# Two-layer adaLN trunk on one core: odd shift blocks of the first stage summed by VectorE, x multiplied by the norm's rows on GpSimd

## The chip, the cores and the metric

The kernel runs on one core of one Trainium2 chip. The metric is the device time of one execution in microseconds (us), as the median of several runs. The engines are named as in the profile: PE (TensorE matmul), PEld (its weight loads), DVE (VectorE), ACT (ScalarE), POOL (GpSimd) and SP (SyncE), which issues the loads.

## The reference

A trunk of two layers over 256 positions and 1024 features, batch 1. Each sub-layer is `x + gate(c) * f(rmsnorm(x) * gain * (1 + scale(c)) + shift(c))`. Layer 0 has block-sparse causal attention with 8 heads of 128 (with 256 positions and blocks of 256 it is one causal block), layer 1 a short gated convolution of width 3; each is followed by a SwiGLU with 2816 hidden features. Shift, scale and gate of each sub-layer are six vectors of 1024 per layer:

```python
sc = jax.nn.silu(c)
for i in range(DEPTH):
    mod = sc @ w_ada[i] + b_ada[i]
    sh_m, sc_m, g_m, sh_f, sc_f, g_f = jnp.split(mod, 6, axis=-1)
    h = modulate(x, norm_mix[i], sh_m, sc_m)   # rms_norm(x, gain) * (1 + scale) + shift
    ...
```

All is float32. The change touches only the first of these: shift and scale of layer 0's mixer, and the h that goes into q and k.

## The kernel before

**Layout.** x is held with features on the 128 partitions, as eight blocks of 128 features x 256 positions (`xT[:, k]`, k = 0 to 7). Matrix products are made in three passes of a split of both operands into a high part (rounded to fp32r) and the rest: `mm3` (lines 252 to 258) issues high x high, high x low and low x high.

**The first stage** (lines 554 to 629) computes q and half of k, 1536 columns, straight from the input. It runs over the eight feature blocks k, not over column chunks, since block k of the normed input h needs shift and scale of block k alone, and these come out of `c` and weights that are still on their way. Six PSUM accumulators (`accs`, four for q, two for k) take 12 groups of three products from each block, 36 products per step.

The order of PE, DVE and ACT is written out by hand here (`manual_schedule`, line 554); POOL and SP are ordered by the framework. In the loop at line 602, step k issues block k's products, with the work for block n = k+1 put in between:

- Loads on SP: the scale block n, the weight rows `wf_qk_n` (lines 138 to 141), and with even n the two shift blocks n and n+1 together. Shift and scale blocks are of 512 KB; two of a kind share one of five 1 MB buffers (tag `wf`), in which the weight rows lie as well. A load waits until the buffer that it gets has been read for the last time. The framework hands the buffers out.
- `scale_column` (line 494): the scale block lies turned, with the output features on the partitions, so one DVE instruction multiplies it by a row of silu(c) that is the same on all partitions (`c_all`) and sums along the free axis (`ada_sum`, line 107). `scale_of` (line 490) then adds the bias and multiplies by the gain.
- `mod_sums` (line 463) for the shift: the block lies with the input features on the partitions, and PE multiplies it by columns of silu(c), to four partial rows. For n = 1 it takes one block (128 columns); for n = 2, 4 and 6 it takes two, n and n+1 (256 columns). ACT copies the rows out of PSUM (line 473), and `mod_columns` (line 476) turns them into a column by products with `firsts`. `shift_columns` (line 484) has ACT add the bias for each column.
- `w_operands` and `operands` (lines 514 and 520): in three pieces of 512 columns, ACT rounds the weight rows to `wh` (line 511) and DVE forms the rest `wl` (line 512).
- `normed` (line 499): DVE forms t = xT x scale column x rows0 in one instruction. `rows0` is the reciprocal root mean square of each position, the same on all partitions.
- `h_operand` (line 504): ACT adds the shift and rounds to `m0h` (line 505), DVE forms the rest `m0l` (line 506).

```python
for k in range(KD):
    n = k + 1
    ...
    first_products(k, ops, range(0, ja))
    if sums:
        y = mod_sums(shifts[:, 1:2] if n == 1 else shifts, f"sh{n}")
    if n < KD:
        scale_column(scales[:, n % 2], n)
    first_products(k, ops, range(ja, jb))
    if n < KD:
        ops_n = w_operands(n, wf)
        if sums:
            shift_columns(y, n)
        t = normed(n)
    first_products(k, ops, range(jb, 6))
    if n < KD:
        operands(n, t, wf, ops_n)
```

So DVE's order for block n is ada_sum, scale_of, wl(0:2), t, m0l, wl(2:4), wl(4:6). In the texts "step n" is this work for block n; PE's products of block n come after it.

After the stage the rest of q, k and v, attention and all further layers follow, with weight chunks of 1 MB split by ACT (line 98) and DVE (line 99), and with further `ada_sum` pieces (line 109) for the later shifts, scales and gates.

Of the kernel before, what the change touches and what calls it, by code (L numbers as in the profile page):

```python
# [11 lines left out]
AF = mybir.ActivationFunctionType  # L12
# [4 lines left out]
S = 256  # L17
# [16 lines left out]
def trunk_kernel(ctx: ExitStack, tc: tile.TileContext, x_t, cols_in, scale_in, shift_in, ada_in, qk_rows, kv_in, o_in,  # L34
# [87 lines left out]
    def mcol(l, part, k):  # L122
        i = l * 48 + part * KD + k
        return mod[:, i:i + 1]
# [20 lines left out]
    def room(tag, n, name, dtype=F32):  # L145
        size = {"al": KF * S + 16, "ah": KF * S, "zh": KD * (S + 32), "zl": KD * (S + 2)}.get(tag, KD * S)
        return act.tile([P, size], dtype, tag=tag, name=name)[:, 16 if tag == "al" else 0:][:, :n]
# [4 lines left out]
    def new_pair(tag, name, nk):  # L152
        return tuple(pair_rows(room(tag + p, nk * S, name + p, F32R)) for p in "hl")

    room("al", 1, "first_al")
    xT = act.tile([P, KD, S], F32, name="xT")
    hs = new_pair("h", "m0", KD)
    room("ah", 1, "first_ah")
# [304 lines left out]
    def mod_sums(w, name):  # L463

        n = w.shape[1]
        ps = ps_misc("mod_ps_" + name)[:, :n * P]
        for k in range(KD):
            g = 32 * (k % 4)
            nc.tensor.matmul(ps[g:g + 32].rearrange("p (n c) -> p n c", c=P), sc[:, k:k + 1].to_broadcast([P, 32]),
                             w[:, :, k * P:(k + 1) * P], start=k < 4, stop=k >= 4, skip_group_check=True,  # L470
                             tile_position=(0, g))
        y = tmp.tile([P, 2 * P], F32, tag="t", name="mod_y_" + name, bufs=3)[:, :n * P]
        nc.scalar.activation(y, ps, AF.Copy)
        return y

    def mod_columns(y, name):

        ps = ps_misc(f"mod_c_{name}")
        n = y.shape[1] // P
        for i in range(n):  # L480
            nc.tensor.matmul(ps[:, i:i + 1], y[:, i * P:(i + 1) * P], firsts, start=True, stop=True)
        return ps[:, :n]

    def shift_columns(y, k):
        ps = mod_columns(y, f"sh{k}")
        for n in range(ps.shape[1]):
            nc.scalar.activation(mcol(0, SH_M, k + n), ps[:, n:n + 1], AF.Identity,
                                 bias=b_cols[:, SH_M * KD + k + n:][:, :1])

    def scale_of(m, k, sums):  # L490

# [2 lines left out]
    def scale_column(w, k):  # L494
        m = mcol(0, SC_M, k)
        ada_sum(m, w, f"sc{k}")
        scale_of(m, k, m)

    def normed(k):
        t = tmp.tile([P, S], F32, tag="t", name=f"t_m0_{k}", bufs=3)  # L500
        nc.vector.scalar_tensor_tensor(t, xT[:, k], mcol(0, SC_M, k), rows0, op0=ALU.mult, op1=ALU.mult)
        return t

    def h_operand(k, t):
# [34 lines left out]
    def keep_warm(n):  # L539

        ps = ps_misc("warm")
        for _ in range(n):
            nc.tensor.matmul(ps[:, :2 * P].rearrange("p (n c) -> p n c", c=P), ident_r,
                             ident_r.unsqueeze(1).to_broadcast([P, 2, P]), start=True, stop=True, skip_group_check=True)
# [9 lines left out]
    with tc.manual_schedule(engines={mybir.EngineType.PE, mybir.EngineType.DVE, mybir.EngineType.Activation}):  # L554
        nc.vector.tensor_copy(ident_r, ident)
        nc.vector.tensor_copy(mask_r, causal)

        std = const.tile([P, 2], F32, name="std0")
        nc.scalar.activation(std[:, :1], eps, AF.Silu)
        keep_warm(4)  # L560
        nc.scalar.activation(sc, c_cols, AF.Silu)
        nc.scalar.activation(std[:, :1], eps, AF.Sqrt)
        b_one = const.tile([P, KD], F32, name="b_one")
        nc.vector.tensor_scalar(b_one, b_cols[:, SC_M * KD:][:, :KD], 1.0, None, op0=ALU.add)
        nc.vector.tensor_scalar(qg, v_cols[:, 56:57], HD ** -0.5, None, op0=ALU.mult)

        c_ps = [ps_alt(f"c_ps_{i}") for i in range(2)]
        for k in range(KD):
            nc.tensor.matmul(c_ps[k // 4][:, k % 4 * P:][:, :P], sc[:, k:k + 1].to_broadcast([P, P]), ident, start=True,
                             stop=True)  # L570
        keep_warm(6)
        sq = room("zl", RAW, "sq0")
        ssq = const.tile([P, 2], F32, name="ssq0")
        nc.scalar.activation(sq[:, :D], x_tok[:, 0], AF.Square, accum_out=ssq[:, 0:1])
        nc.vector.scalar_tensor_tensor(sq[:, D:2 * D], x_tok[:, 1], 1.0, x_tok[:, 1], op0=ALU.mult, op1=ALU.mult,
                                       accum_out=ssq[:, 1:2])
        for i in range(2):
            nc.scalar.activation(c_all[:, i * 512:(i + 1) * 512], c_ps[i], AF.Copy)
        nc.scalar.activation(std, ssq, AF.Sqrt, bias=eps, scale=1.0 / D)
        rstd0 = const.tile([P, 2], F32, name="rstd0")  # L580
        nc.vector.reciprocal(rstd0, std)
        x_ps = turn_x(0, ps_alt)
        nc.vector.tensor_copy(xT[:, 0:2], x_ps)
        y = mod_sums(scales[:, 0:1], "sc0")
        rr0 = rstd_rows(rstd0, "rr_0")
        rows0 = tmp.tile([P, S], F32, tag="rrow", name="rows0", bufs=1)
        nc.scalar.activation(rows0, rr0, AF.Copy)
        x_ps = turn_x(1, ps_alt)
        ps = mod_columns(y, "sc0")
        scale_of(mcol(0, SC_M, 0), 0, ps)  # L590
        y = mod_sums(shifts[:, 0:1], "sh0")
        t = normed(0)
        nc.vector.tensor_copy(xT[:, 2:4], x_ps)
        keep_warm(2)
        ops = w_operands(0, wf)
        shift_columns(y, 0)
        x_ps = [turn_x(i, ps_alt) for i in (2, 3)]
        operands(0, t, wf, ops)
        for i in range(2):
            nc.scalar.activation(xT[:, 4 + 2 * i:6 + 2 * i], x_ps[i], AF.Copy)  # L600
        keep_warm(4)
        for k in range(KD):
            n = k + 1
            if n < KD:
                if n % 2 == 0:
                    shifts, scales = ada_first(n // 2)
                    load_first(shifts, shift_in, n)
                    load_first(shifts, shift_in, n + 1)
                elif n == 1:
                    load_first(shifts, shift_in, 1)  # L610
                load_first(scales, scale_in, n)
                wf = first_rows(n)
            ja, jb = ((2, 3), (1, 2), (1, 4), (0, 3))[min(k, 3)]
            sums = n < KD and (n == 1 or n % 2 == 0)
            first_products(k, ops, range(0, ja))
            if sums:
                y = mod_sums(shifts[:, 1:2] if n == 1 else shifts, f"sh{n}")
            if n < KD:
                scale_column(scales[:, n % 2], n)
            first_products(k, ops, range(ja, jb))  # L620
            if n < KD:
                ops_n = w_operands(n, wf)
                if sums:
                    shift_columns(y, n)
                t = normed(n)
            first_products(k, ops, range(jb, 6))
            if n < KD:
                operands(n, t, wf, ops_n)
                ops = ops_n
# [193 lines left out]
def _lay_out(inputs):  # L823

    import numpy as np

    a = {k: np.asarray(v) for k, v in inputs.items()}

    def feats(v):
        return v.reshape(-1, P).T  # L830

    def chunks(w):

        k, j = w.shape[0] // P, w.shape[1] // CW
        return w.reshape(k, P, j, CW).transpose(2, 1, 0, 3).reshape(j, P, k * CW)

    ada = a["w_ada"].reshape(DEPTH, D, 6, KD, P)
    turned = ada.transpose(0, 2, 3, 4, 1)
    qkv = a["w_qkv"][0]

    def sums(part):

        return ada[0, :, part].reshape(KD, P, KD, P).transpose(2, 1, 0, 3).reshape(KD, P, D)

    return {
        "x_tok": a["x"][0].reshape(2, P, D).transpose(1, 0, 2),
        "cols": np.concatenate([feats(a[n]) for n in ("b_ada", "norm_mix", "norm_ffn", "conv_w", "q_gain", "k_gain", "c")],
                               axis=1),
        "scale": np.concatenate([sums(SC_M)[:1], turned[0, SC_M, 1:]]),
        "shift": sums(SH_M),  # L850
        "ada": turned.reshape(DEPTH, 6, 4, 2, P, D).transpose(0, 1, 2, 4, 3, 5).reshape(DEPTH, 6, 4, P, 2 * D),
        "qk_rows": qkv[:, :D + D // 2].reshape(KD, P, D + D // 2),
        "kv": chunks(qkv[:, D + D // 2:]),
        "o": chunks(a["w_o"][0]),
        "in": chunks(a["w_in"][0]),
        "out": chunks(a["w_out"][0]),
        "gate_up": np.stack([chunks(w) for w in a["w_gate_up"]]),
        "down": np.stack([chunks(w) for w in a["w_down"]]),
    }
# [21 lines left out]
```

## Time and profile before

| | us |
|---|---|
| median of 3 runs (586.2 to 587.33) | 587.23 |
| the profiled execution, its own time | 586.6 |
| its span in the trace | 584.8 |
| PE busy | 577.4 (99%) |
| DVE busy | 454.8 (78%) |
| ACT busy | 316.1 (54%) |
| POOL busy | 1.1 |

The span is what the trace covers; 1.8 us of the execution lie around it. Starts are in us from the start of the span. A row of the timeline gives start, duration, engine, line, operation, written and read tiles, their shapes and count, and in brackets an idle time before it with what ended it. Durations of instructions that follow each other on an engine overlap a little, so the distance between two starts is what an instruction costs its engine.

### The profile page before, as it was taken

What the parts mean: (1) busy time and instruction counts of PE and PEld (TensorE: products, weight loads), DVE (VectorE), ACT (ScalarE), POOL (GpSimd) and SP (SyncE); (2) the same over time, 40 slices, a digit from 0 to 9 for tenths busy, and PEclk for the clock granted to TensorE, in tenths of its full rate; (3) what the DMA queues carried; (4) which work ended last, traced back from release to release, by engine and by line L of the source; (5) the groups of instructions that cost most, each with busy time, mean ns of one, the idle gap of its engine ahead of it and who ended that gap; (6) DMA issues with size and microseconds to landing.
All of it is one profiled execution on the core that took longest, in us unless ns stands there. A gap on an engine that the chain in (4) does not pass through costs nothing.

```text
span 584.8 us, 12020 instructions
## 1 busy us (share of the span) xinstructions
PE 577.4 (99%) x5032; PEld 569.8 (97%) x5032; DVE 454.8 (78%) x722; ACT 316.1 (54%) x526; POOL 1.1 (0%) x8
## 2 busy tenths in 40 slices
PE   7999999999999999999999999999999999999997
PEld 6899999999999999999999999999999999999997
DVE  4789989999999798967977999759986576555550
ACT  6457889597644454544445745446745345443330
POOL 0000000000000000000000000000000000000000
PEclk9999999999999999999999999999999999999999
DMA  8999999955898999968986379637387566655400
GB/s 316 396 380 409 356 331 334 341 208 187 335 377 303 347 334 342 331 240 303 330 310 254 129 291 366 247 122 261 128 331 280 180 261 216 238 174 200 148 19 18
DMA packets 25109, 156.04 MB, mean 267 GB/s; under 512 B 2784, under 2 KB 3168, under 8 KB 8928
## 3 DMA queue, kind: packets, MB, share of 16 engines
q1 hardware_dynamic: 25056, 155.28, 71.8%
q8 instruction: 39, 0.64, 0.4%
q14 instruction: 14, 0.11, 0.0%
HBM read 154.22 MB, written 1.05 MB: 266 GB/s over the span
## 4 chain that ended last, share of the span: by engine, by line
PE 93%; DMA 2%; DVE 2%; ACT 1%; issue 1%; SPq 0%; ACTq 0%; DVEq 0%
PE pu L255 7%; PE pu L254 7%; PE pu L258 7%; PE op_d L255 6%; PE op_d L254 6%; PE op_d L258 6%; PE pg L254 6%; PE pg L258 6%; PE pg L255 6%; PE raw_f L254 1%; PE op_o L258 1%; PE raw_f L255 1%; PE raw_f L258 1%; PE pb L258 1%; PE pb L254 1%; PE op_o L254 1%
## 5 line engine op out<-in xcount | busy, mean ns | idle before, releaser
L109 DVE SCALAR_TENSOR_TENSOR prod<-wa,c_all 128x1024 f32<-128x1024 f32 x80 | 97.6, 1220 | 18.0 <-DMA wa<-in_ada_dram 17.2
L98 ACT ACTIVATE wh_d<-wf_d 128x1024 fp32r<-128x1024 f32 (+1 forms) x48 | 45.2, 981 | 62.6 <-issue 41.9
L99 DVE TENSOR_TENSOR wl_d<-wf_d,wh_d 128x1024 fp32r<-128x1024 f32 (+1 forms) x48 | 52.8, 1132 | 23.9 <-ACT wh_d L98 23.7
L98 ACT ACTIVATE wh_g<-wf_g 128x1024 fp32r<-128x1024 f32 x44 | 45.7, 1053 | 44.6 <-issue 44.2
L98 ACT ACTIVATE wh_u<-wf_u 128x1024 fp32r<-128x1024 f32 x44 | 44.6, 1051 | 36.1 <-issue 30.5
L99 DVE TENSOR_TENSOR wl_u<-wf_u,wh_u 128x1024 fp32r<-128x1024 f32 x44 | 52.3, 1220 | 13.6 <-ACT wh_u L98 13.3
L99 DVE TENSOR_TENSOR wl_g<-wf_g,wh_g 128x1024 fp32r<-128x1024 f32 x44 | 53.5, 1219 | 2.4 <-ACT wh_g L98 2.2
L254 PE MATMUL op_d<-a0h,wh_d 128*128 128x256 f32 x176 | 48.6, 276 | 0.0
L258 PE MATMUL op_d<-a0h,wl_d 128*128 128x256 f32 x176 | 48.6, 276 | 0.0
L255 PE MATMUL op_d<-a1l,wh_d 128*128 128x256 f32 x176 | 48.6, 276 | 0.0
L254 PE MATMUL op_d<-a1h,wh_d 128*128 128x256 f32 x176 | 48.6, 276 | 0.0
L255 PE MATMUL op_d<-a0l,wh_d 128*128 128x256 f32 x176 | 48.6, 276 | 0.0
L258 PE MATMUL op_d<-a1h,wl_d 128*128 128x256 f32 x176 | 48.6, 276 | 0.0
L254 PE MATMUL pg<-f0h,wh_g 128*128 128x256 f32 x160 | 44.5, 278 | 0.0
L258 PE MATMUL pg<-f0h,wl_g 128*128 128x256 f32 (+3 forms) x164 | 44.5, 275 | 0.0
L254 PE MATMUL pg<-f1h,wh_g 128*128 128x256 f32 x160 | 44.3, 277 | 0.0
L255 PE MATMUL pg<-f0l,wh_g 128*128 128x256 f32 x160 | 44.2, 276 | 0.0
L254 PE MATMUL pu<-f0h,wh_u 128*128 128x256 f32 x160 | 44.2, 276 | 0.0
L258 PE MATMUL pg<-f1h,wl_g 128*128 128x256 f32 x160 | 44.2, 276 | 0.0
L258 PE MATMUL pu<-f1h,wl_u 128*128 128x256 f32 x160 | 44.2, 276 | 0.0
L255 PE MATMUL pu<-f0l,wh_u 128*128 128x256 f32 x160 | 44.2, 276 | 0.0
L255 PE MATMUL pg<-f1l,wh_g 128*128 128x256 f32 x160 | 44.2, 276 | 0.0
(294 smaller groups left out, 2022.8 us busy)
## 6 DMA issues: line engine op xcount, KB each, us to landing
wa<-in_ada_dram SPq DMA_DIRECT2D x40, 1024.0 KB, 6.8
wf_g<-in_gate_up_dram SPq DMA_DIRECT2D x22, 1024.0 KB, 5.3
wf_u<-in_gate_up_dram SPq DMA_DIRECT2D x22, 1024.0 KB, 4.9
wf_d<-in_down_dram SPq DMA_DIRECT2D x16, 1024.0 KB, 6.1
wf_d<-in_down_dram SPq DMA_DIRECT2D x8, 768.0 KB, 5.3
wa_sc<-in_scale_dram SPq DMA_DIRECT2D x8, 512.0 KB, 6.9
wa_sh<-in_shift_dram SPq DMA_DIRECT2D x8, 512.0 KB, 7.9
wf_qk<-in_qk_rows_dram SPq DMA_DIRECT2D x8, 512.0 KB, 6.7
```

Of the source, the lines that this page charges most:

```text
L98: nc.scalar.activation(wh[:, a:b], wf[:, a:b], AF.Copy)
L99: nc.vector.tensor_sub(wl[:, a:b], wf[:, a:b], wh[:, a:b].bitcast(F32))
L109: nc.vector.scalar_tensor_tensor(t, w, 1.0, c_all, op0=ALU.mult, op1=ALU.mult, accum_out=dst)
L254: nc.tensor.matmul(ps, ah, bh, start=first, stop=False, skip_group_check=True)
L255: nc.tensor.matmul(ps, ah, bl, start=False, stop=False, skip_group_check=True)
L258: nc.tensor.matmul(ps[:, a:b], al, bh[:, a:b], start=False, stop=last, skip_group_check=True)
```

## The change

Shift blocks with odd n are laid out turned in memory, as the scale blocks are, and DVE sums them with `ada_sum`, ahead of the scale's. Shift blocks with even n stay on PE, one block (128 columns) at a time, and n = 1 leaves PE. A new tile `xn` holds x times rows0 for blocks 1 to 7; POOL makes these products once, ahead of the loop. `normed` for blocks 1 to 7 becomes one ACT instruction that multiplies `xn` by the scale column; block 0 keeps the DVE instruction. `shift_of` adds the shift's bias on ACT for one column. `xn` takes the place of a one-column placeholder in the buffer `al`, which attention uses later.

```diff
-    room("al", 1, "first_al")
+    xn = pair_rows(room("al", KD * S, "xn"))
...
+    def shift_of(k, sums):
+        nc.scalar.activation(mcol(0, SH_M, k), sums, AF.Identity, bias=b_cols[:, SH_M * KD + k:][:, :1])
+
     def shift_columns(y, k):
-        ps = mod_columns(y, f"sh{k}")
-        for n in range(ps.shape[1]):
-            nc.scalar.activation(mcol(0, SH_M, k + n), ps[:, n:n + 1], AF.Identity,
-                                 bias=b_cols[:, SH_M * KD + k + n:][:, :1])
+        shift_of(k, mod_columns(y, f"sh{k}"))
...
     def normed(k):
         t = tmp.tile([P, S], F32, tag="t", name=f"t_m0_{k}", bufs=3)
-        nc.vector.scalar_tensor_tensor(t, xT[:, k], mcol(0, SC_M, k), rows0, op0=ALU.mult, op1=ALU.mult)
+        if k == 0:
+            nc.vector.scalar_tensor_tensor(t, xT[:, k], mcol(0, SC_M, k), rows0, op0=ALU.mult, op1=ALU.mult)
+        else:
+
+            nc.scalar.activation(t, xn[:, k], AF.Copy, scale=mcol(0, SC_M, k))
         return t
...
             nc.scalar.activation(xT[:, 4 + 2 * i:6 + 2 * i], x_ps[i], AF.Copy)
+        for k in range(1, KD):
+            nc.gpsimd.tensor_mul(xn[:, k], xT[:, k], rows0)
         keep_warm(4)
...
-            sums = n < KD and (n == 1 or n % 2 == 0)
+
+            sums = n < KD and n % 2 == 0
             first_products(k, ops, range(0, ja))
             if sums:
-                y = mod_sums(shifts[:, 1:2] if n == 1 else shifts, f"sh{n}")
+                y = mod_sums(shifts[:, 0:1], f"sh{n}")
             if n < KD:
+                if n % 2:
+                    ada_sum(mcol(0, SH_M, n), shifts[:, 1], f"sh{n}")
                 scale_column(scales[:, n % 2], n)
             first_products(k, ops, range(ja, jb))
             if n < KD:
                 ops_n = w_operands(n, wf)
                 if sums:
                     shift_columns(y, n)
+                else:
+                    shift_of(n, mcol(0, SH_M, n))
                 t = normed(n)
...
-        "shift": sums(SH_M),
+        "shift": np.stack([turned[0, SH_M, k] if k % 2 else sums(SH_M)[k] for k in range(KD)]),
```

## Rows read from the trace of the kernel before

**Rows 1.** The page: the span, the busy time of each engine with its share of the span, and of the 40 slices the lines for PE's granted clock and for DMA, in tenths.

```profile
span 584.8 us, 12020 instructions
PE 577.4 (99%) x5032; PEld 569.8 (97%) x5032; DVE 454.8 (78%) x722; ACT 316.1 (54%) x526; POOL 1.1 (0%) x8
...
PEclk9999999999999999999999999999999999999999
DMA  8999999955898999968986379637387566655400
```

**Rows 2.** Busy time by stretch: the stretch in us and its length, busy time of PE, PEld, DVE, ACT and POOL with the number of instructions, PE's granted clock, the share of DMA and GB/s.

```profile
20.00:25.00 5.00, 5.00 (x51) 4.42 (x43) 2.94 (x6) 2.26 (x7) 0.00 (x0) 1.00 1.03 405
25.00:30.00 5.00, 4.95 (x48) 4.57 (x51) 4.26 (x10) 2.23 (x6) 0.00 (x0) 1.00 1.02 375
...
50.00:60.00 10.00, 10.00 (x90) 8.78 (x89) 9.79 (x12) 9.56 (x22) 0.00 (x0) 1.00 1.01 411
```

**Rows 3.** The chain that ended last, from 15 to 26 and from 49 to 54 us: start, time on the chain, what.

```profile
15.41 6.78 DMA wf_qk<-in_qk_rows_dram
...
22.21 0.64 ACT wh_qk L511
...
24.60 0.49 DVE m0l L506
...
25.14 0.39 PE pq L255
...
49.58 0.20 PE pq L255
...
53.69 0.57 PE q_sums L661 x8
```

**Rows 4.** The timeline of DVE in the first stage: the ada_sum of step 1 and of step 2, the whole step 3 up to the ada_sum of step 4, and m0l of step 7.

```profile
14.42 1.23 DVE L109 SCALAR_TENSOR_TENSOR prod_sc<-wa_sc,c_all 128x1024 f32<-128x1024 f32 x1
...
20.93 1.23 DVE L109 SCALAR_TENSOR_TENSOR prod_sc<-wa_sc,c_all 128x1024 f32<-128x1024 f32 x1 [1.02 <-DMA wa_sc<-in_scale_dram]
...
26.33 1.22 DVE L109 SCALAR_TENSOR_TENSOR prod_sc<-wa_sc,c_all 128x1024 f32<-128x1024 f32 x1
27.47 0.08 DVE L109 DVE_READ_ACCUMULATOR prod_sc<-wa_sc,c_all 128x1 f32 x1
27.59 0.22 DVE L492 SCALAR_TENSOR_TENSOR mod<-mod,b_one,cols 128x1 f32<-128x1 f32 x1
27.73 0.68 DVE L512 TENSOR_TENSOR wl_qk<-wf_qk,wh_qk 128x512 fp32r<-128x512 f32 x1
28.33 0.48 DVE L501 SCALAR_TENSOR_TENSOR t_m<-xT,mod,rows 128x256 f32<-128x256 f32 x1
29.44 0.48 DVE L506 SCALAR_TENSOR_TENSOR m0l<-t_m,mod,m0h 128x256 fp32r<-128x256 f32 x1 [0.64 <-ACT m0h L505]
...
31.17 1.22 DVE L109 SCALAR_TENSOR_TENSOR prod_sc<-wa_sc,c_all 128x1024 f32<-128x1024 f32 x1
...
48.85 0.48 DVE L506 SCALAR_TENSOR_TENSOR m0l<-t_m,mod,m0h 128x256 fp32r<-128x256 f32 x1 [0.64 <-ACT m0h L505]
```

**Rows 5.** ACT: from its timeline rows0, the shift columns of step 2, m0h of step 3 and, from attention's k, an accumulator read and the instruction that reads what it wrote; and of line 338 in the later layers the durations in ns (least, median, most), first and last start.

```profile
9.76 0.38 ACT L587 ACTIVATE rows<-rr 128x256 f32<-128x256 f32 x1
...
22.75 0.39 ACT L487 ACTIVATE mod<-mod_c_sh,cols 128x1 f32<-128x1 f32 x2
...
28.90 0.51 ACT L505 ACTIVATE m0h<-t_m,mod 128x256 fp32r<-128x256 f32 x1 [2.77 <-DVE t_m L501]
...
68.66 0.22 ACT L643 ACTIVATION_READ_ACCUMULATOR sqh<-pk 128x1 f32 x1
68.92 0.30 ACT L646 ACTIVATE sd<-ss,eps 128x4 f32<-128x4 f32 x1
...
L338 ACT ACTIVATE a0h<-xT,mod x8: 494/496/513, 117.5 to 130.7; 128x256 fp32r<-128x256 f32 x8
```

**Rows 6.** The timeline of PE: mod_sums and columns of the shift, the narrow form of step 1 and the wide form of step 4.

```profile
14.70 0.64 PE L469 MATMUL mod_ps_sh<-wa_sh,sc 128*32 128x128 f32 x16
...
16.09 0.28 PE L481 MATMUL mod_c_sh<-firsts,mod_y_sh 128*128 128x1 f32 x2
...
29.41 1.07 PE L469 MATMUL mod_ps_sh<-wa_sh,sc 128*32 128x256 f32 x16
...
32.64 0.50 PE L481 MATMUL mod_c_sh<-firsts,mod_y_sh 128*128 128x1 f32 x4
```

**Rows 7.** The timelines of POOL and DVE at the start: POOL's last instruction, and two casts of the same form on DVE.

```profile
1.35 0.29 POOL L77 TENSOR_SCALAR_AFFINE_SELECT causal<-causal 128x128 f32<-128x128 f32 x1
...
1.43 0.29 DVE L555 CAST ident_r<-ident 128x128 fp32r<-128x128 f32 x1
1.68 0.23 DVE L556 CAST mask_r<-causal 128x128 fp32r<-128x128 f32 x1
```

**Rows 8.** Two loads as SP issued them, each with the time from its issue to its landing: the scale of step 4, and the first piece of the weight rows of step 6 (durations in ns, then first and last start).

```profile
L132 SPq DMA_DIRECT2D wa_sc<-in_scale_dram x1: 327/327/327, 21.0 to 21.0; - x1
DMA to landing us min/median/max: 9.0/9.0/9.0
...
L140 SPq DMA_DIRECT2D wf_qk<-in_qk_rows_dram x1: 328/328/328, 36.1 to 36.1; - x1
DMA to landing us min/median/max: 4.1/4.1/4.1
```

## The prediction

> **What bounds it now.** The page comes first [rows 1]: TensorE (PE) is busy 577.4 of 584.8 us, the granted clock is full in every slice, and DMA is near its most in the first eight slices. So any time lost or won in the first stage stays lost or won: behind it PE has hardly a gap in which to catch up. An average over the span says nothing of who paces the first stage, so the next view is busy time by stretch [rows 2]. From 25 to 30 us PE is full, VectorE (DVE) has 4.26 of 5 us, DMA 1.02. Three resources are all close to their limit there, and ScalarE (ACT, 2.23) and GpSimd (POOL, nothing) are the only ones with room. From 50 to 60 us DVE is at 9.79 of 10.
>
> The chain that ended last tells who is truly waited for [rows 3]. It goes through the load of the weight rows wf_qk_2 (issued 15.41, landed before 22.21), then wh, the normed tile, m0h and m0l of step n=2, and reaches PE at 25.14. From there to the end of the stage it stays on PE. But PE's lead is thin. In step 7 m0l starts at 48.85 and takes 0.48 [rows 4]; the product that needs it is on the chain at 49.58 [rows 3]. PE is 0.2 us behind DVE after six steps.
>
> DVE's own step is the third view [rows 4]. Call T the start of ada_sum for the scale. ada_sum with its accumulator read and hand-over takes 1.26 (26.33 to 27.59), wl(0:2) follows at 27.73, the normed tile at 28.33, and m0l at 29.44 after waiting for m0h; the next T is 31.17. So m0l starts at T+3.11 and the step is 4.84, of which 1.73 lies behind the start of m0l. Steps 3 to 7 repeat this without any external wait: **DVE paces itself at 4.84**. PE needs 35 products from 49.58 to 53.69 [rows 3], 0.1175 each, so 4.23 for a step of 36; every second step adds mod_sums (1.07) and its columns (0.50) [rows 6], less some overlap, so about 4.9 on average. The two are level.
>
> **The change on PE.** Step 1 loses mod_sums and columns (0.64 + 0.28 [rows 6]); steps 2, 4 and 6 go from the wide to the narrow forms, at most 1.07 - 0.64 and 0.50 - 0.28 each, 0.65. In all 0.9 + 3 x 0.65 = 2.9 us at most leave PE, some 2.6 with the overlaps. This is worth something only while PE is last.
>
> **The change on DVE.** Steps 1, 3, 5 and 7 gain an ada_sum, 4 x 1.26 = 5.0 us. Steps 1 to 7 lose the normed tile (0.48 each [rows 4], 3.4 us). But a DVE step is not a sum of busy times, because m0l waits for ACT. The normed tile now runs on ACT, in front of m0h and behind scale_of, so the two ACT instructions stand in series. Its price: the same form, a copy of 128x256 with a column as scale, takes 0.494 to 0.496 at L338 [rows 5]; I take 0.50. m0h starts 0.09 after the tile it reads is done (28.33 + 0.48 to 28.90 [rows 4, 5]); I take that for DVE to ACT. An ACT instruction that reads what the one before wrote starts 0.04 after its end (68.66 + 0.22 to 68.92 [rows 5]); between ACT and DVE I take 0.03 (28.90 + 0.51 to 29.44).
>
> Even step: scale_of ends at T + 1.26 + 0.22 = T+1.48; the tile runs T+1.57 to 2.07, m0h 2.11 to 2.62, m0l starts at T+2.65; the step is 2.65 + 1.73 = **4.38**, 0.46 shorter. wl(0:2) fits into the wait. Odd step, counted from the ada_sum of the shift: all is 1.26 later, m0l at T+3.91, and the step is **5.64**, 0.80 longer. A pair takes 10.02 against 9.68: DVE gets slower as PE gets lighter.
>
> **The sum.** Step 1 starts at 14.42 as before [rows 4]; 14.42 + 5.64 = 20.06, and the scale of step 2 is only there at 20.93, so the longer first step is covered with 0.87 to spare (without this wait it would cost 0.8). Step 2 still waits for wf_qk_2: wh ends at 22.85 [rows 3], the shift's activation starts at 22.75 and holds ACT some 0.17 (two took 0.39 [rows 5]), so the tile starts at 22.92 and m0l at 22.92 + 0.50 + 0.04 + 0.51 + 0.03 = 24.00, 0.60 earlier than 24.60. Then T3 = 25.73, T4 = 31.37, T5 = 35.75, T6 = 41.39, T7 = 45.77, and m0l of step 7 starts at 49.68 where it was 48.85. PE takes its first product with an m0l 0.54 after the start of m0l (24.60 to 25.14 [rows 3]): 50.22 against 49.58, **0.64 us later**. PE itself would be ready for that step some 1.3 us earlier, so its 2.6 us go into new waits for m0l. What follows on DVE (full from 50 us) moves along.
>
> Bounds. If ACT's two instructions overlap by 0.09, as independent ones do, in place of standing 0.04 apart, each of six steps gains 0.13 and the sum is -0.15. If hand-overs are 0.1 longer it is +1.2. I take 0.64, from the rows of the very forms.
>
> **Covered costs.** ACT gains 7 x 0.5 us; from 20 to 30 us it was idle for over half of the time [rows 2]. Behind its wait for scale_of stand m0h and the last two wh pieces, which DVE wants only after m0l. POOL has seven products, each of two inputs. The nearest row is a select of 128x128 in 0.29 [rows 7]; twice the elements is 0.58, and at twice that for the second input 1.16. The tile for step 1 is wanted at about 17, the one for step 7 after 47; rows0 is there by 10.2 [rows 5], so 7 x 1.16 = 8.1 us are in time, and nothing stands behind them in POOL's queue. The loads keep their sizes and SP order, but a shift tile is now given back by an ada_sum in the odd step, not by mod_sums in the even one. The scale of step 4, issued at 20.97 and landed 9.0 us later [rows 8], will get a later slot, freed about 25.7 to 27.0. With the shortest flight seen, 4.1 [rows 8], it lands between 29.8 and 31.1; it is wanted at 31.37. This cover is the thinnest; each us that it is late costs one.
>
> **POOL beside DVE.** No row shows POOL arithmetic beside a DVE instruction of two inputs. The nearest pair is a DVE cast of 0.29 that overlaps POOL's select, against 0.23 for the same cast behind it [rows 7]: 0.06 more. Seven such are 0.4, inside the 0.87 spare. At the other end each of the six POOL products after the first holds DVE for its whole 0.58. I take the nearest row, so nothing; the other end is a rival. The Trainium skill ("SBUF — State Buffer", Who interferes with whom) speaks for that other end: a VectorE instruction with two SBUF inputs and a GpSimd one that reads SBUF share a port, and the one that starts first keeps it throughout. The overlapping cast has one input, so no run here shows this rule at work; by it the sum would be that of the rival.
>
> **The rivals.**
> 1. POOL blocks DVE (slower). Place: 11 to 20 us, where DVE runs two-input instructions almost without a gap. 6 x 0.58 = 3.5, less the 0.87 spare and the 0.65 for which DVE waits for m0h in step 1, puts T2 at 20.93 + 2.0 = 22.9. Then m0l of step 2 starts at 25.58 in place of 24.00, and the sum is 0.64 + 1.58 = +2.2. It decides once DVE is held for over 1.5 us in all. Against it: the cast's 0.06.
> 2. PE is last after all (faster). If ACT hands over so quickly that DVE keeps ahead, PE runs from 24.54 through 6 x 4.23 and two sums of some 0.8 to 51.5, against 53.69: -2.1. Against it: DVE's step has no outside wait that could shrink.
> 3. Loads come late. If the slots freed later let the scale or the weight rows of steps 4 or 6 miss their steps by a us in all, it is +0.64 + 1.0 = +1.6.
> 4. The overlap bound with all else right: -0.15, no change to measure; it belongs to the forecast.
>
> **How the numbers follow.** The profiled run took 586.6; the sum is 587.2 on it. The median shown is 587.23, 0.6 above it, so 587.23 + 0.64 = 587.9 is the time. Something under 0.2% (1.2 us) can't be told from no change here. Forecast 0.50 (-0.2 to +1.2, all within 0.2%); rival 1 0.27 and rival 3 0.08, both slower; rival 2 0.15, faster. So faster 0.15, same 0.50, slower 0.35. The forecast's own range is 587.0 to 588.4. The whole range, 585.6 to 589.7, takes in rival 1 at 589.4 with some spread, and the smaller gains of rival 2; the full -2.1 and longer holds of POOL stay out.
>
> **What would show it.** Right: odd steps of DVE near 5.6 and even ones near 4.4 from about 21 us, m0l of step 2 near 24.0, PE waiting for m0l before odd steps, stage end near 54.3. Rival 1: prod_sh, prod_sc or wl longer than their 1.2 and 0.7 between 12 and 20 us, or POOL products far over 0.6, and step 2 starting after 21. Rival 2: no PE wait for m0l and step 7's products before 48. Rival 3: DVE or ACT idle on wa_sc or wf_qk in steps 4 or 6. The forecast is wrong if a DVE pair takes under 9.7 or the stage ends before 53.

## The result, and the profile after

The changed kernel takes 590.12 us (589.88 to 591.53, 4 runs) against 586.94 for the kernel before: a ratio of 1.0056, interval 1.0034 to 1.0078. It is slower by some 3.2 us, where 0.7 was forecast and 589.7 was the upper end. The profiled run took 591.53.

The page of the changed kernel: PE's busy time is hardly changed, POOL appears, and PE's granted clock has a slice at 7 tenths, which it had nowhere in [rows 1].

```profile
span 589.8 us, 11989 instructions
...
PE 579.1 (98%) x5008; PEld 571.7 (97%) x5008; DVE 459.7 (78%) x723; ACT 319.7 (54%) x532; POOL 9.1 (2%) x15
...
PEclk9799999999999999999999999999999999999999
```

Busy time by stretch, with the columns of [rows 2]: from 20 to 25 us the clock is 0.58 where it was 1.00, from 25 to 30 us 0.74, and DMA falls to 0.53.

```profile
13.00:20.00 7.00, 4.80 (x39) 4.40 (x38) 6.93 (x9) 2.91 (x7) 6.37 (x6) 1.00 1.02 386
20.00:25.00 5.00, 4.09 (x27) 3.22 (x28) 3.67 (x8) 2.66 (x6) 0.00 (x0) 0.58 1.05 383
25.00:30.00 5.00, 5.00 (x35) 5.00 (x34) 3.44 (x7) 2.79 (x7) 0.00 (x0) 0.74 0.53 196
```

The timeline of POOL: the first product takes 0.72, two beside DVE 2.00, four 5.32.

```profile
10.37 0.72 POOL L606 TENSOR_TENSOR xn<-xT,rows 128x256 f32<-128x256 f32 x1 [8.71 <-ACT rows L591]
12.05 2.00 POOL L606 TENSOR_TENSOR xn<-xT,rows 128x256 f32<-128x256 f32 x2 [0.96 <-DVE xT L597]
14.38 5.32 POOL L606 TENSOR_TENSOR xn<-xT,rows 128x256 f32<-128x256 f32 x4 [0.33 <-ACT xT L604]
```

DVE in the same time and after it, to be set against [rows 4]. While POOL runs, m0l of block 0 takes 0.65 where it took 0.48, ada_sum takes 1.76 and 1.64 where it took 1.23, scale_of 0.56 where it took 0.22, two wl pieces 2.36 where two take 1.29 (the last row of step 1 below, with POOL done). m0l of step 1 starts at 20.89, 2.8 us later than before, and step 2 at 22.62 in place of 20.93.

```profile
12.81 0.65 DVE L510 SCALAR_TENSOR_TENSOR m0l<-t_m,mod,m0h 128x256 fp32r<-128x256 f32 x1 [0.23 <-ACT m0h L509]
13.38 2.36 DVE L516 TENSOR_TENSOR wl_qk<-wf_qk,wh_qk 128x512 fp32r<-128x512 f32 x2
15.67 1.76 DVE L109 SCALAR_TENSOR_TENSOR prod_sh<-wa_sh,c_all 128x1024 f32<-128x1024 f32 x1
...
17.47 1.64 DVE L109 SCALAR_TENSOR_TENSOR prod_sc<-wa_sc,c_all 128x1024 f32<-128x1024 f32 x1
...
19.15 0.56 DVE L492 SCALAR_TENSOR_TENSOR mod<-mod,b_one,cols 128x1 f32<-128x1 f32 x1
...
20.89 0.49 DVE L510 SCALAR_TENSOR_TENSOR m0l<-t_m,mod,m0h 128x256 fp32r<-128x256 f32 x1 [0.58 <-ACT m0h L509]
21.41 1.29 DVE L516 TENSOR_TENSOR wl_qk<-wf_qk,wh_qk 128x512 fp32r<-128x512 f32 x2
22.62 1.22 DVE L109 SCALAR_TENSOR_TENSOR prod_sc<-wa_sc,c_all 128x1024 f32<-128x1024 f32 x1
...
26.96 0.48 DVE L510 SCALAR_TENSOR_TENSOR m0l<-t_m,mod,m0h 128x256 fp32r<-128x256 f32 x1 [1.49 <-ACT m0h L509]
...
28.69 1.22 DVE L109 SCALAR_TENSOR_TENSOR prod_sh<-wa_sh,c_all 128x1024 f32<-128x1024 f32 x1
...
34.35 1.22 DVE L109 SCALAR_TENSOR_TENSOR prod_sc<-wa_sc,c_all 128x1024 f32<-128x1024 f32 x1
```

PE waits 3.05 us for step 1, the first product after it takes 0.58, and the sums of q, which end the stage, start at 58.95.

```profile
20.91 0.58 PE L254 MATMUL pq<-m0h,wh_qk 128*128 128x256 f32 x1 [3.05 <-ACT m0h L509]
...
58.95 0.64 PE L672 MATMUL q_sums<-qsq,one 128*32 128x256 f32 x8
```

In the kernel before, m0l of step 1 and the sums of q are these rows:

```profile
18.10 0.48 DVE L506 SCALAR_TENSOR_TENSOR m0l<-t_m,mod,m0h 128x256 fp32r<-128x256 f32 x1 [0.64 <-ACT m0h L505]
...
53.62 0.64 PE L661 MATMUL q_sums<-qsq,one 128*32 128x256 f32 x8
```

The chain that ended last shows what a product costs after that wait: 0.21 each, against 0.1175 before.

```profile
22.23 0.21 PE pq L254
22.44 0.21 PE pq L255
22.66 0.21 PE pq L258
```

ACT, which now forms the tile t, stands first in line behind PE's shift column (step 2) and later behind a load (step 6):

```profile
25.72 0.26 ACT L485 ACTIVATE mod<-mod_c_sh,cols 128x1 f32<-128x1 f32 x1 [0.97 <-PE mod_c_sh L481]
25.88 0.50 ACT L505 ACTIVATE t_m<-xn,mod 128x256 f32<-128x256 f32 x1
...
46.70 0.63 ACT L515 ACTIVATE wh_qk<-wf_qk 128x512 fp32r<-128x512 f32 x1 [1.85 <-DMA wf_qk<-in_qk_rows_dram]
```

### The profile page after: what moved, and what is told of

Same layout as the page of the kernel before. It is cut to its first block, busy times and chain, and to the rows that moved or that the text cites. A ratio compares the mean times of both kernels' runs of the same rounds, so it can differ in the third digit from the quotient of the medians.

```text
span 589.8 us, 11989 instructions
## 1 busy us (share of the span) xinstructions
PE 579.1 (98%) x5008; PEld 571.7 (97%) x5008; DVE 459.7 (78%) x723; ACT 319.7 (54%) x532; POOL 9.1 (2%) x15
## 4 chain that ended last, share of the span: by engine, by line
PE 90%; DVE 4%; DMA 2%; ACT 2%; issue 2%; SPq 0%; DVEq 0%; ACTq 0%
PE pu L254 7%; PE pu L258 7%; PE pu L255 7%; PE op_d L254 6%; PE op_d L255 6%; PE op_d L258 6%; PE pg L254 6%; PE pg L258 6%; PE pg L255 6%; PE raw_f L254 1%; PE raw_f L255 1%; PE raw_f L258 1%; PE pb L258 1%; PE pb L254 1%; PE pv L255 1%
## 5 line engine op out<-in xcount | busy, mean ns | idle before, releaser
L258 PE MATMUL pu<-f0h,wl_u 128*128 128x256 f32 x160 | 44.2, 276 | 0.0
```

What stands on the lines that cost most here:

```text
L258: nc.tensor.matmul(ps[:, a:b], al, bh[:, a:b], start=False, stop=last, skip_group_check=True)
```

## The experiments

Two theories were set against each other. **A**: POOL's products hold DVE's instructions of two inputs; PE then waits so long that its clock falls, and the late PE holds ACT and DVE in turn. **B**: the shift tile given back later makes loads late, and POOL does not matter. The stage end below is always the start of q_sums on PE; before it is 53.62.

**The change without POOL's products.** ACT forms t from x itself, so this kernel leaves out the factor rows0 for blocks 1 to 7; it is there for its timing.

```diff
-            nc.scalar.activation(t, xn[:, k], AF.Copy, scale=mcol(0, SC_M, k))
+            nc.scalar.activation(t, xT[:, k], AF.Copy, scale=mcol(0, SC_M, k))
...
-        for k in range(1, KD):
-            nc.gpsimd.tensor_mul(xn[:, k], xT[:, k], rows0)
```

> The change without POOL's seven products: ACT forms the tile from x itself, so the factor of the norm's rows is left out of blocks 1 to 7. Theory A (POOL's products hold DVE's two-input instructions from 11 to 20 us; PE then waits 3 us and its clock falls): prod_sh and prod_sc are back at 1.2 us each, m0l of step 1 starts near 18.3 (20.9 in the changed kernel), the ada_sum of step 2 at 20.9, m0l of step 2 near 24.0, granted clock 1.00 throughout, m0l of step 7 near 49.7 or up to 1 later if loads are late; 587.5 to 588.6 us. Theory B (the loads that get their buffers later make the loss, POOL does not matter): the step 1 instructions may shorten, but ACT still waits for wf_qk in steps 5 to 7 and the time stays within 0.5 us of 590.1.

Measured: 587.92 us, ratio to before 1.0018 (1.0006 to 1.0029), against 1.0056 with POOL; the clock was at 0.999 to 1.000 in every run. Its DVE:

```profile
14.81 1.22 DVE L109 SCALAR_TENSOR_TENSOR prod_sh<-wa_sh,c_all 128x1024 f32<-128x1024 f32 x1
16.08 1.23 DVE L109 SCALAR_TENSOR_TENSOR prod_sc<-wa_sc,c_all 128x1024 f32<-128x1024 f32 x1
18.68 0.48 DVE L510 SCALAR_TENSOR_TENSOR m0l<-t_m,mod,m0h 128x256 fp32r<-128x256 f32 x1 [0.52 <-ACT m0h L509]
...
23.88 0.48 DVE L510 SCALAR_TENSOR_TENSOR m0l<-t_m,mod,m0h 128x256 fp32r<-128x256 f32 x1 [0.40 <-ACT m0h L509]
25.61 1.22 DVE L109 SCALAR_TENSOR_TENSOR prod_sh<-wa_sh,c_all 128x1024 f32<-128x1024 f32 x1
...
31.21 1.22 DVE L109 SCALAR_TENSOR_TENSOR prod_sc<-wa_sc,c_all 128x1024 f32<-128x1024 f32 x1
...
35.55 1.22 DVE L109 SCALAR_TENSOR_TENSOR prod_sh<-wa_sh,c_all 128x1024 f32<-128x1024 f32 x1
...
41.15 1.22 DVE L109 SCALAR_TENSOR_TENSOR prod_sc<-wa_sc,c_all 128x1024 f32<-128x1024 f32 x1
...
46.40 1.22 DVE L109 SCALAR_TENSOR_TENSOR prod_sh<-wa_sh,c_all 128x1024 f32<-128x1024 f32 x1
```

and its stage end on PE:

```profile
55.12 0.64 PE L670 MATMUL q_sums<-qsq,one 128*32 128x256 f32 x8
```

A holds. The odd step is 31.21 - 25.61 = 5.60 and the even one 35.55 - 31.21 = 4.34: the prediction's step arithmetic (5.64 and 4.38) stands. Step 6 takes 46.40 - 41.15 = 5.25, 0.9 more than an even step (ACT waits 2.33 us for its wf_qk): there B's late load is real as well. The stage ends at 55.12, +1.5: 0.9 of it is the load, and the 0.6 that is left is what the prediction gave to the longer chain (0.64).

**The change with PE kept busy in its wait.**

```diff
+            if k == 0:
+                keep_warm(24)
             if n < KD:
                 operands(n, t, wf, ops_n)
```

> The change with 24 idle products (2.8 us) on PE behind the products of block 0, where PE waited 3.05 us. Theory A: DVE's part stays (m0l of step 1 near 20.9, ada_sum of step 2 near 22.6), but the granted clock stays at 1.00, the products of block 1 run at 0.12 and not 0.21 us each, m0l of step 2 starts near 25.3 and not 27.0, and the time is 1 to 1.7 us under the changed kernel's, 588.4 to 589.1. If the clock is not what makes even steps longer: no change, 590.1 within 0.3.

Measured: 588.88 us, ratio 1.0035 (1.0003 to 1.0066). m0l of step 1 starts at 20.96, the hold by POOL is as in the change; but the clock stays full in the first stage, and m0l of step 2 starts at 25.35, not 26.96:

```profile
25.35 0.48 DVE L510 SCALAR_TENSOR_TENSOR m0l<-t_m,mod,m0h 128x256 fp32r<-128x256 f32 x1 [0.58 <-ACT m0h L509]
...
56.55 0.64 PE L674 MATMUL q_sums<-qsq,one 128*32 128x256 f32 x8
```

```profile
20.00:25.00 5.00, 4.71 (x47) 3.98 (x47) 4.12 (x8) 3.70 (x9) 0.00 (x0) 1.00 1.00 376
...
300.00:350.00 50.00, 48.28 (x407) 48.03 (x406) 43.51 (x78) 29.13 (x45) 0.00 (x0) 0.97 0.64 228
```

The stage ends at 56.55. The only edit is work for PE in a time in which it had none, so what it wins (1.0 us against the repeated change below, 2.4 against the first profile) is the clock's part. The interval of the whole time overlaps the change's; the trace of the first stage decides this one.

The second row is a warning. The profiled run took 591.9, and its clock over the whole run is 0.997: far behind the stage, at about 318 us, the clock falls, and just before that PE has waited 1.72 us for DVE (the tile ss_n). One more of the eight runs is at 0.997 (591.38); the six at 0.999 or 1.000 took 588.14 to 589.42. In the kernel before 3 of the 24 runs beside this one were at 0.997 as well (590.02 to 593.91). So a clock below 1 over a whole run does not by itself say that it fell in the first stage.

**One part alone: the sums.** `normed` stays on DVE, no POOL product, `ada_sum` for odd shift blocks as in the change.

```diff
-            nc.scalar.activation(t, xn[:, k], AF.Copy, scale=mcol(0, SC_M, k))
+            nc.vector.scalar_tensor_tensor(t, xT[:, k], mcol(0, SC_M, k), rows0, op0=ALU.mult, op1=ALU.mult)
```

> One part alone: the odd shift blocks are summed on DVE, but the normed tile stays one DVE instruction; no POOL product. By the step arithmetic of the prediction odd steps of DVE take 4.84 + 1.26 = 6.10 and even ones 4.84, so m0l of step 7 starts at 52.6 against 48.85 before, +3.7 us: 590.4 to 591.0. If DVE does not pace the stage (PE does): within 0.5 us of before or faster. Granted clock 1.00 in both.

Measured: 593.34 us, ratio 1.0114 (1.0098 to 1.0131). The direction is right and odd steps take the 6.1 expected (6.11), but the loss is 6.5, not 3.7. In the profiled run (592.32) the stage ends at 58.51, 4.9 late. m0l of step 7 starts at 53.70, of which 1.2 is a wl_k piece of the next stage that the framework put in front of it, and the rest of DVE's order behind the stage changed too. The clock was not at 1.00, as expected, in every run: 0.999 in the profiled one, 0.996 or 0.997 in the other three (593.09 to 595.13), and no trace shows where those three lost it. DVE paces the stage; the size was not foreseen.

**The other part alone: the norm.** Shift sums on PE as before, t by POOL and ACT.

```diff
-            sums = n < KD and n % 2 == 0
+            sums = n < KD and (n == 1 or n % 2 == 0)
...
-                if n % 2:
-                    ada_sum(mcol(0, SH_M, n), shifts[:, 1], f"sh{n}")
```

> The other part alone: shift sums stay on PE as before, the normed tile of blocks 1 to 7 goes to POOL and ACT. Theory A: POOL still holds DVE between 11 and 19 us, but with one ada_sum less m0l of step 1 starts near 19.5 and PE waits about 1 us there, so the clock stays at 1.00; DVE's steps are 4.4, PE paces the rest with 4.9; the time is -0.6 to +0.8 us of before, 586.3 to 587.8. Theory B (no buffer is given back later here): no late load, and a time under before by 0.3 to 0.6. If a wait of 1 us on PE is enough to lower the clock: 1 to 2 us above before.

Measured: 588.26 us, ratio 1.0024 (1.0005 to 1.0044), 0.5 over the expected range. The stage ends at 54.02, only 0.4 late; another 1.1 of the span is lost behind it, and by what was not followed. The clock is full in the trace (one of the ten runs was at 0.997), and ACT waits at most 0.5 for the weight rows of steps 4 and 6. There m0l waits 1.75, not 0.6, since ACT has the shift's column ahead of t, and the column waits for PE:

```profile
34.82 0.48 DVE L512 SCALAR_TENSOR_TENSOR m0l<-t_m,mod,m0h 128x256 fp32r<-128x256 f32 x1 [1.75 <-ACT m0h L511]
```

**The change again**, in one group with the next three.

> The changed kernel once more, beside its variants. 589.9 to 590.3 us median. Both theories: POOL beside DVE as before; PE waits 3 us before block 1. If the loss of clock decides how long it takes, runs differ among themselves with the granted clock.

Measured: 590.15 us (12 runs), ratio 1.0044 (1.0019 to 1.0068). Its granted clock was 0.994 to 0.997 in all 12 runs, 589.29 to 590.41 where it was 0.996 or 0.997 and 590.60 to 591.20 where it was 0.994. In the profile (589.86, at 0.997) the clock falls in the same place as in the first one:

```profile
20.00:25.00 5.00, 4.08 (x33) 3.55 (x34) 3.93 (x8) 3.07 (x8) 0.00 (x0) 0.78 1.02 392
25.00:30.00 5.00, 5.00 (x41) 5.00 (x40) 4.20 (x8) 2.49 (x6) 0.00 (x0) 0.88 0.73 247
```

```profile
57.52 0.64 PE L672 MATMUL q_sums<-qsq,one 128*32 128x256 f32 x8
```

PE waits 3.11 us here and 3.05 in the first profile, yet the loss differs. Read by single us, the clock is at half from about 22.8 to 26.2 here, two us after PE has begun again, and from about 20.8 to 27.6 in the first profile. So the loss of clock in the stage is in both profiles of this kernel, and the first, at 0.994, shows the larger form. The other 14 runs of this kernel have no trace.

**POOL's products paced**: a ring of two tiles, so that a product starts when ACT has read the one two before it.

```diff
+        def times_rows(k):
+            xns[k] = tmp.tile([P, S], F32, tag="xn", name=f"xn_{k}", bufs=2)
+            nc.gpsimd.tensor_mul(xns[k], xT[:, k], rows0)
...
                 ops = ops_n
+                if n + 2 < KD:
+                    times_rows(n + 2)
```

> The change with POOL's products in a ring of two tiles, so that product n+2 can start only when ACT has read product n: two run at the start, the others in the time for which DVE waits for m0h. Theory A (POOL holds DVE's two-input instructions): prod_sh and prod_sc of step 1 back near 1.2 us, m0l of step 1 near 18.6 to 19.3, ada_sum of step 2 at 20.9, clock 1.00; m0l in steps 1 to 5 up to 0.2 longer; m0l of step 7 at 50 to 51.5 with the late load of step 6; 587.9 to 589.0 us. If the number of POOL products matters and not what they lie beside: as the changed kernel, 590.1.

Measured: 588.03 us, ratio 1.0023 (0.9994 to 1.0051). The interval overlaps that of the change, but 11 of the 12 runs (587.06 to 589.22) lie under every run of the change (589.29 and more). All seven products are there, but five of them run about the time for which DVE waits for m0h. m0l of step 1 starts at 18.38, that of step 7 at 50.15, the stage ends at 54.91, the clock is at 0.999 to 1.000. What matters is what the products lie beside, not their number:

```profile
17.88 0.73 POOL L609 TENSOR_TENSOR xn<-xT,rows 128x256 f32<-128x256 f32 x1 [4.83 <-ACT t_m L505]
```

```profile
18.38 0.51 DVE L510 SCALAR_TENSOR_TENSOR m0l<-t_m,mod,m0h 128x256 fp32r<-128x256 f32 x1 [0.57 <-ACT m0h L509]
...
50.15 0.48 DVE L510 SCALAR_TENSOR_TENSOR m0l<-t_m,mod,m0h 128x256 fp32r<-128x256 f32 x1 [0.58 <-ACT m0h L509]
```

**Without POOL, the sums of 3, 5 and 7 a step earlier**, so that the shift tile is given back as early as before. This kernel too leaves out the factor rows0 for blocks 1 to 7.

```diff
-                if n % 2:
-                    ada_sum(mcol(0, SH_M, n), shifts[:, 1], f"sh{n}")
+                odd = 1 if n == 1 else n + 1
+                if n == 1 or n % 2 == 0 and odd < KD:
+                    ada_sum(mcol(0, SH_M, odd), shifts[:, 1], f"sh{odd}")
```

> As the run without POOL's products (the factor of the norm's rows is left out of blocks 1 to 7), but the shift blocks 3, 5 and 7 are summed one step earlier, in the even step, so that the shift tile is given back as early as before the change. Theory of late loads: ACT's wait for wf_qk of step 6 (0.9 us on the path) goes, and step 7 has no sum of its own: m0l of step 7 starts near 48.4 to 48.9 (50.27 without this edit), the stage ends near 53.3; 586.3 to 587.2 us, at or under before. If the wait for wf_qk comes from the loads themselves and not from when the tile is given back: the wait stays, only the 1.26 us of step 7 is won, 586.6 and over.

Measured: 587.76 us, ratio 1.0007 (0.9986 to 1.0028), 0.6 over the expected range. Step 6 takes 45.44 - 39.84 = 5.60 with its sum, as long as step 4 with its (35.51 - 29.91), so the late load is gone: it came from when the tile is given back.

```profile
39.84 1.22 DVE L109 SCALAR_TENSOR_TENSOR prod_sh<-wa_sh,c_all 128x1024 f32<-128x1024 f32 x1
...
45.44 1.22 DVE L109 SCALAR_TENSOR_TENSOR prod_sc<-wa_sc,c_all 128x1024 f32<-128x1024 f32 x1
```

m0l of step 7 starts at 48.04 and the stage ends at 52.81, 0.8 ahead of before. Yet the total is no better: behind the stage the framework now puts two q tiles ahead of wl_k on DVE, and PE waits for v's weights, which it did nowhere before:

```profile
PE pv L255 <- DVE wl_v L99: 0.9, 1, 0.9
PE pv L254 <- ACT wh_v L98: 0.5, 1, 0.5
```

**POOL's products beside the kernel before**, read by nothing.

```diff
+        for k in range(1, KD):
+            nc.gpsimd.tensor_mul(xn[:, k], xT[:, k], rows0)
         keep_warm(4)
```

> The kernel before with POOL's seven products added, which nothing reads: the disputed cost by itself. Theory A: DVE's two-input instructions between 11 and 19 us are held, some 2.5 us in all, m0l of step 1 starts at 19.5 to 20.5 (18.10 before); the wait for the scale of step 2 takes up about 1 us of it; 587.2 to 588.2 us with the clock at 1.00. If a shared port costs nothing: m0l of step 1 at 18.1 and no change of time.

Measured: 589.07 us, ratio 1.0025 (0.9998 to 1.0053), 0.9 over the expected range. The times scatter (587.30 to 591.44), and four of the 12 runs had a clock of 0.993 to 0.997, which was not expected and which no trace shows. So the times leave no change open. The trace, at full clock (PE waits 1.32 us for step 1), does not: ada_sum is held by 0.5 and m0l of step 1 is 1.5 us late, though no result of POOL is used.

```profile
15.08 1.76 DVE L109 SCALAR_TENSOR_TENSOR prod_sc<-wa_sc,c_all 128x1024 f32<-128x1024 f32 x1
...
19.57 0.48 DVE L506 SCALAR_TENSOR_TENSOR m0l<-t_m,mod,m0h 128x256 fp32r<-128x256 f32 x1 [0.64 <-ACT m0h L505]
```

**Both cures together**: products paced and sums a step earlier, on the whole computation.

> The change with POOL's products paced (a ring of two) and the shift blocks 3, 5, 7 summed one step earlier; the whole computation. Theory A with late loads: no hold of DVE before 20 us, clock 1.00, m0l of step 7 near 48.2, stage end near 53.0, under before's 53.6; but the order in which the framework puts DVE's work behind the stage is that of the run with earlier sums, where PE waited 1.4 us for wl_v, so 587.5 to 588.0 us in all. If the waits for wl_v there had another cause than this order: 585.8 to 586.3.

Measured: 588.07 us, ratio 1.0022 (1.0009 to 1.0035). The stage ends at 53.56, no later than before and 0.6 later than expected; m0l of step 7 starts at 48.73. PE waits 0.9 and 0.5 for v's weights again.

**And the order behind the stage kept** as the kernel before has it:

```diff
+    with tc.manual_schedule(engines={mybir.EngineType.DVE, mybir.EngineType.Activation}):
+        produce(0)
+        for j in range(2):
+            q_features(j, accs[j])
+        produce(1)
+        q_features(2, accs[2])
     ahead = get(("k", 2))
-    for j in range(3):
-        q_features(j, accs[j])
```

> The same, with the first work of DVE and ACT behind the stage written out in the order that the kernel before has there (wl_k, two q tiles, wl_k, a q tile). Theory: the stage's gain of 0.6 to 0.8 us over before is kept, 585.8 to 586.4 us. If DVE or ACT is full there whatever the order: 587 to 588.

Measured: 586.41 us, ratio 0.9992 (0.9981 to 1.0003): the whole loss is taken back, and no gain over before can be claimed. The stage ends at 53.42, 0.2 ahead of before and not 0.6 to 0.8. The waits for v's weights are gone. DVE in this kernel:

```profile
48.60 0.48 DVE L510 SCALAR_TENSOR_TENSOR m0l<-t_m,mod,m0h 128x256 fp32r<-128x256 f32 x1 [0.58 <-ACT m0h L509]
...
50.59 2.36 DVE L99 TENSOR_TENSOR wl_k<-wf_k,wh_k 128x1024 fp32r<-128x1024 f32 x2 [0.18 <-ACT wh_k L98]
```

## Why the prediction was wrong, point by point

**The step that failed** is "POOL beside DVE": "I take the nearest row, so nothing". The nearest row, a DVE cast of one input beside a select [rows 7], was not near enough. DVE's instructions of two inputs are held: m0l of block 0, the two wl pieces behind it, two ada_sums and a scale_of together take 2.5 us more than without POOL. Whether the second input or the other POOL instruction makes the difference to the cast, no run separates. The rule of the Trainium skill ("SBUF — State Buffer", Who interferes with whom), that such an instruction and a reading GpSimd one exclude each other on a shared port, is borne out by these rows in kind. In size they stay under it: ada_sum is held by 0.41 to 0.53, where the first POOL product takes 0.72, and six products of 0.72 would be 4.3 us where 2.5 were lost.

**Rival 1** therefore happened, at its own place and nearly at its price: step 2 starts at 22.62 where it gave 22.9, and with the clock full (PE kept busy) m0l of step 2 starts at 25.35 where it gave 25.58. That its price came so near is partly luck, since two errors offset each other: it put the hold at 3.5 us and not 2.5, and it took off 0.65 for DVE's wait for m0h, which absorbed nothing (m0l of step 1 still waits 0.58). The hold costs 1.4 us of the stage (56.55 against 55.12). It got a chance of 0.27.

**What no case held** is the clock. The rival moved step 1 but did not ask what PE does meanwhile: in the first profile it waits 3.05 us and comes back at 0.21 per product in place of 0.1175; the clock is at 0.58 and 0.74 in the next two stretches. PE then reaches mod_columns late, ACT holds t behind the shift's column, and DVE's even steps grow from 4.34 to 6.07 (step 2) and 5.40 (step 4). This costs 1.0 us in the repeated run and 2.4 in the first profile.

**The DVE and ACT chain** was right: 5.60 and 4.34 measured against 5.64 and 4.38, m0l of step 2 at 23.88 against 24.00. So was its consequence: with POOL out of the way the time is +1.1 us over before and not under it, late load included. In this order of DVE's work PE's 2.6 us were worth nothing, as argued.

**The covered loads** were wrong in place and right in kind. The load named as thinnest, the scale of step 4, was in time; the weight rows of step 6 were late, by 0.9 us in the run without POOL and by about 0.4 in the change (step 6 at 4.78 in place of 4.34). This is rival 3, and it came together with rival 1: cases that were given separate chances were not exclusive.

The account at the stage end, for the repeated run: 57.52 - 53.62 = 3.9 us. The clock is 57.52 - 56.55 = 1.0, the hold 56.55 - 55.12 = 1.4, the late load and the longer chain 55.12 - 53.62 = 1.5. These are differences between traces, and each is good to a few tenths: m0l of block 0 starts 0.2 later in the trace with PE kept busy than in that of the change, and the load of step 6 is late by 0.9 without POOL, 0.7 with PE kept busy and 0.4 in the change. The span grew by 588.1 - 584.8 = 3.3; 0.6 is won back behind the stage, and by which wait was not followed.

## What to carry to other kernels

Work put on an idle engine is not free: here GpSimd's products slowed VectorE's two-input instructions beside them, though the two engines wrote different tiles. Count the new instructions that fall beside such a neighbour and price each at its own length, unless a row shows otherwise. Here that price was 4.3 us and the hold 2.5. Where PE is the bound, ask of every delay how long PE will stand still by it: a wait of some 3 us cost another 1.0 and 2.4 us in clock here. Rivals that do not exclude each other should be added up, not only listed.

## What the runs showed that was not expected

- The clock was below full in each of the 16 runs of the changed kernel (0.994 to 0.997 over the whole run), with a wait of 3.05 and 3.11 us in its two profiles. It stayed at 0.999 or 1.000 in every run of five variants (the change without POOL, paced, with earlier sums, with both, and with the order kept), and their profiles show PE waiting under 0.9 us at a time in the stage. The sums alone, without POOL, do not fit in: three of the four runs were at 0.996 or 0.997, with waits of 1.2 us in the stage in the one that was profiled, at 0.999. The kernel before fell to 0.996 or 0.997 in 7 of 35 runs too, and where was not traced.
- Pacing alone is worth 2.1 us (590.15 to 588.03): a ring of two tiles, which makes POOL wait for ACT, moved five of its products into DVE's waits, where m0l grew from 0.48 to at most 0.53.
- What the framework does behind a stage can undo a gain in it: 0.8 us ahead at the stage end became 1.0 behind in the span (585.8 against 584.8), by an order of DVE's and ACT's work that cost PE 1.4 us of waits. Written out as before for both engines, these waits are gone; which of the two orders mattered was not tried.
